# Streaming the columns of each linear product in one of seven orders

## The chip, the cores and the metric

One core of a Trainium2 chip runs the whole kernel. The metric is device time in microseconds. TensorE multiplies a stationary operand (128 x 128, loaded ahead of the matmul) with columns that are streamed from SBUF, and adds the result in PSUM. VectorE, ScalarE and GpSimd work beside it, and SyncE's queue starts most DMA transfers.

## What is computed

Three layers on a sequence of 256 tokens with 2048 features, all in float32: a block with stick-breaking attention and a gated delta rule, cross-attention to a memory and a convolutional feed-forward part; then a block with forgetting attention; then one with windowed attention. Between them stand normalisations and residual additions. Nearly all the arithmetic is in products of the hidden state with weight matrices:

```python
h = rmsnorm(x, mix_norm[l])
proj = h @ w_in[l]
...
x = x + mixed @ w_out[l]
...
u = causal_dwconv(h @ w_up, conv_w) + conv_b
gate, up = jnp.split(u, 2, axis=-1)
return (jax.nn.silu(gate) * up) @ w_down
...
p = h @ fox_w_in[j]
```

## The kernel before

The hidden state lies transposed in SBUF (`XT`, features on partitions, 256 tokens along the free axis). A float32 operand is split in two parts that TensorE takes in one pass each: a rounded high part and the rest, the low part. For x, `split` (line 211) leaves both in one tile `mv[P, 2, 256]`: high in `mv[:, 0, :]`, low in `mv[:, 1, :]`. For the weights, `granules` (line 242) loads blocks of up to four k-tiles of 256 weight columns by SyncE's queue into `wt`, lets ScalarE round them (line 262) and VectorE subtract (line 263), and hands out high and low weights of one k-tile after the other. It calls `tick` after each block of k-tiles, which lets waiting side work (attention, norms, the delta rule) put its own instructions between.

`linB` (line 270) makes one product of 256 output columns. For each k-tile and each half `j` of the 256 columns it issues a pair of matmuls. The first holds the high weights still and streams 512 columns: x high and x low, into `ps[:, j]`, which is one PSUM bank of 2 x 256 words. The second holds the low weights still, streams the 256 columns of x high, and adds them to the second half of the same bank, `ps[:, j, 1, :]`. The two halves are added when the result leaves PSUM (`scaled`, line 290, or `residual`, line 339). The accumulator `ps` has two buffers in turn. Most products have 16 k-tiles, so 32 pairs; those with `w_down` have 11, those with `w_xo` 4.

`linA` (line 280) does the same with x stationary and the weights streamed. The change does not touch it.

Instructions stand on each engine in the order in which the program text issues them; no planner moves them. Every matmul goes through `mm` (line 139), so all of them carry line 140 in the profile (`PE ... L140`), and VectorE's helpers carry lines 151 and 154. Groups are therefore told apart by the tiles they read and write: `linb<-xh,w` is a product of `linB` on the normalised hidden state, `linb<-mv,w`, `linb<-mix,w` and `linb<-mm,w` are those on other inputs.

A few smaller places are named below. `scores` (line 1048) makes the attention scores `zps` from `kd` and `qs`; its last matmul streams two runs of 128 columns that lie 256 apart, the other two stream 256 in a row. Line 604 makes `kq` with streamed columns in two runs of 64; `gbc` (line 599) streams 128 in a row. In `head`, line 768 makes `zps<-bset,identb`, writing 256 columns of PSUM as two runs of 128 that lie 256 apart. Lines 655 to 661, in the loop over `LEVELS = (2, 4, 8, 16, 32)`, write tile `X` from `xps` on VectorE: 128 elements of each partition, in runs of 2, 4, 8, 16 or 32 by the level, at both ends.

Of the kernel before, what the change touches and what calls it, by code (L numbers as in the profile page):

```python
# [24 lines left out]
FFC = 11  # L25
ROT = [(i + 8) % 16 if i < 16 else i for i in range(32)]
LEVELS = (2, 4, 8, 16, 32)

def _consts():
# [15 lines left out]
    parts["m0c"] = (q64 == r64 + 1) & (r64 % 2 == 0)  # L47
    for b in LEVELS:
        m = (r64 // (2 * b) == q64 // (2 * b)) & ((r64 // b) % 2 == 1) & ((q64 // b) % 2 == 0)
# [74 lines left out]
def body(ctx: ExitStack, tc: tile.TileContext, d: dict, out: bass.AP, stop=None):  # L124
# [14 lines left out]
    def mm(o, lhsT, rhs, start, stop):  # L139
        nc.tensor.matmul(o, lhsT, rhs, start=start, stop=stop, skip_group_check=True)  # L140

    def side(shape, name):
        t = pside.tile([P, 512], F32, tag="side", name=name)
        n = int(np.prod(shape[1:]))
        v = t[:, :n]
        if len(shape) == 3:
            v = v.rearrange("p (a b) -> p a b", a=shape[1])
        return v

    def tt(o, a, b, op):  # L150
        vec.tensor_tensor(o, a, b, op=op)  # L151
# [29 lines left out]
    ps = side([P, 2, P], "warm")  # L181
# [43 lines left out]
    def tick():  # L225

        for lane, width in WIDTH.items():
            for gen in list(lanes.get(lane, ()))[:width]:
                if next(gen, "end") == "end":
                    lanes[lane].remove(gen)  # L230
# [11 lines left out]
    def granules(w, runs, c0, first=(), inner=False):  # L242

        flat = []
        for r0, mvs in runs:
            g = 0
            for n in first:
                flat.append((r0 + g, mvs[g : g + n]))
                g += n
            for g in range(g, len(mvs), KG):  # L250
                flat.append((r0 + g, mvs[g : g + KG]))
        for gi, (r, mvs) in enumerate(flat):
            wt = wp.tile([P, len(mvs), 256], F32, tag="wt", name="wt", bufs=NWT)
            assert c0 % 256 == 0
            src = w[c0 // 2 : c0 // 2 + P, r * 256 : (r + len(mvs)) * 256].rearrange("p (k n) -> p k n", n=256)
            nc.sync.dma_start(wt[:], src)
            for h in range(0, len(mvs), KC):
                n = min(KC, len(mvs) - h)
                part = [mv() if callable(mv) else mv for mv in mvs[h : h + n]]
                w2 = wp.tile([P, n, 2, 256] if inner else [P, 2, n, 256], F32R, tag="w2", name="w2", bufs=NWC)  # L260
                wh, wl = (w2[:, :, e, :] if inner else w2[:, e] for e in range(2))
                act(wh, wt[:, h : h + n, :], AF.Copy)  # L262
                tt(wl, wt[:, h : h + n, :], wh.bitcast(F32), ALU.subtract)
                for i in range(n):
                    last = gi == len(flat) - 1 and h + i == len(mvs) - 1
                    both = w2[:, i] if inner else w2[:, :, i, :]
                    yield both, part[i], gi == 0 and h + i == 0, last
                tick()

    def linB(w, runs, c0, first=()):  # L270

        ps = pl.tile([P, 2, 2, 256], F32, tag="lin", name="linb")
        for w2, mv, first, last in granules(w, runs, c0, first):
            for j in range(2):
                c = slice(j * P, (j + 1) * P)
                mm(ps[:, j], w2[:, 0, c], mv[:], first, False)
                mm(ps[:, j, 1, :], w2[:, 1, c], mv[:, 0, :], False, last)
        return ps

    def linA(w, runs, c0):  # L280

        ps = pl.tile([P, 2, 2, 256], F32, tag="lin", name="lina")
        for w2, mv, first, last in granules(w, runs, c0, inner=True):
            for r in range(2):
                c = slice(r * P, (r + 1) * P)
                mm(ps[:, r], mv[:, 0, c], w2, first, False)
                mm(ps[:, r, 1, :], mv[:, 1, c], w2[:, 0, :], False, last)
        return ps
# [89 lines left out]
    def residual(w, runs, scale=1.0, after=None):  # L378

        for n in range(0, KT, 2):  # L380
            ps = linB(w, runs, n * P)
            xt = XT[:, n : n + 2, :]
            for e in range(2):
                stt(xt, ps[:, :, e, :], scale, xt, ALU.mult, ALU.add)
            if after is not None:
                after(n)
                after(n + 1)
# [149 lines left out]
    def gdn(hp):  # L537
        nonlocal r1, c1
        KQ = gd.tile([P, 2, 2, 256], F32, tag="KQ", name="KQ")
        if hp:  # L540
            for qk, seg in ((1, 0), (0, 1)):
                silu(KQ[:, qk], conv(linB(win, [(0, xh)], 3072 + 1024 * seg + 256 * hp), 8 * seg + 2 * hp))
        else:
            pq = linB(win, [(0, xh)], 3072, (2, 2, 4, 4, 4))
            norm0 = Norm("mix")
            later("norm", squares(norm0))
            r1 = norm0.rstd(0)
            pk = linB(win, [(0, xh)], 4096, (4, 4))
            nc.sync.dma_start(cols[:, 16:], d["cols"][:, 16:])
            tg = thin(d["w_gates"], V("mix_norm"))  # L550
        ps = linB(win, [(0, xh)], 5120 + 256 * hp)
        if hp == 0:
            silu(KQ[:, 1], conv(pq, 0))
            silu(KQ[:, 0], conv(pk, 8))
            nc.sync.dma_start(cst[:], d["consts"])
            late_constants()
            c1 = column(r1)
            later("gdn", make_gates(tg))
        v = conv(ps, 16 + 2 * hp)
        silu(v[:], v)  # L560
        ps = linB(win, [(0, xh)], 6144 + 256 * hp)
        z = t2("y", "z", 2)
        scaled(z[:], ps, r1)
        sz = t2("sz", "sz", 2)
        silu(sz[:], z)
        later("gdn", chain(hp, KQ, v, sz))

    def chain(hp, KQ, v, sz):
# [70 lines left out]
        act(T[:], tps, AF.Copy)  # L639
        for b in LEVELS:  # L640
            nb = 32 // b
# [6 lines left out]
            def product(lhsT, rhs, name):  # L648
                ps = side([P, 4, 64], name)
                for u in range(4):  # L650
                    for f in range(2):
                        mm(ps[HALF[f], u], lhsT[HALF[f], u], rhs[HALF[f], u], u == 0, u == 3)
                return ps
# [9 lines left out]
            nps = product(X, TT, "nps2")  # L663
            if b != LEVELS[-1]:
                mps = product(TT, X, "mps")
# [127 lines left out]
    def new_mv():  # L793
        return mvbox[0].tile([P, 2, 256], F32R, tag="mv", name="mv")
# [25 lines left out]
    with tc.tile_pool(name="xa", bufs=2) as xa_:  # L820
# [51 lines left out]
        for n in range(2):  # L872
            ps = linB(wkv, [(0, mmv)], n * 256)
# [33 lines left out]
    with tc.tile_pool(name="ff", bufs=2) as ff_:  # L907
# [15 lines left out]
        for n in range(22):  # L923
# [6 lines left out]
            for j in range(2):  # L930
                mv = new_mv()
# [96 lines left out]
    def halves(src, tag, bufs):  # L1028

        st = [ap_.tile([P, 2, 256], F32R, tag=f"{tag}{e}", name=tag, bufs=bufs) for e in range(2)]  # L1030
        for e in range(2):
            act(st[e][HALF[e]], src[HALF[e]], AF.Copy)
        for e in range(2):
            tt(st[e][HALF[1 - e]], src[HALF[e]], st[e][HALF[e]].bitcast(F32), ALU.subtract)
        return st
# [82 lines left out]
    for gidx in range(8):  # L1118
        c0 = 256 * gidx
        q = ap_.tile([P, 2, 256], F32, tag="qk", name="q")  # L1120
        k = ap_.tile([P, 2, 256], F32, tag="qk", name="k")
        vr = ap_.tile([P, 2, 256], F32, tag="v", name="v", bufs=1)
        ps = linB(wfx, [(0, xh)], c0)
        scaled(q[:], ps, r5, 0.125)
        q = halves(q, "qs", 1)
        if gidx == 0:
            c5 = column(r5)
        ps = linB(wfx, [(0, xh)], 2048 + c0)
# [11 lines left out]
        ps = linA(wfx, [(0, xh)], 4096 + c0)  # L1140
# [15 lines left out]
    def roped(ps, scale, tag):  # L1156
        qs = ap_.tile([P, 2, 256], F32, tag="gp", name="qs")
        scaled(qs[:], ps, r6, scale)
        rp = ap_.tile([P, 2, 256], F32, tag="rp", name="rp", bufs=1)
        vec.stream_shuffle(rp[:].rearrange("p a b -> p (a b)"), qs[:].rearrange("p a b -> p (a b)"), ROT)  # L1160
        o = ap_.tile([P, 2, 256], F32, tag=tag, name="ro")
        t = rp
        gps.tensor_tensor(t[:], rp[:], L("sin").unsqueeze(1).to_broadcast([P, 2, 256]), op=ALU.mult)
        tt(o[:], qs[:], L("cos").unsqueeze(1).to_broadcast([P, 2, 256]), ALU.mult)
        tt(o[:], o[:], t[:], ALU.add)
        return o
# [16 lines left out]
    ps = linA(wsw, [(0, xh)], 2304)  # L1183
    rows_scaled(lambda r: vr[:, r, :], ps, c6)
    ymv = [None] * KT
    for gidx in range(8):
        kvh = gidx // 2
        q = halves(roped(linB(wsw, [(0, xh)], 256 * gidx), 0.125, "qk"), "qs", 1)
# [59 lines left out]
def build(arrays, stop=None):  # L1248
    import concourse.bacc as bacc

    nc = bacc.Bacc("TRN2", target_bir_lowering=False, num_devices=1)
    d = {n: nc.dram_tensor(f"in_{n}", a.shape, F32, kind="ExternalInput").ap() for n, a in arrays.items()}
    out = nc.dram_tensor("out_0", (D, S), F32, kind="ExternalOutput").ap()
    with tile.TileContext(nc) as tc:
        body(tc, d, out, stop)
    return nc
# [9 lines left out]
```

## Time and profile before

| | us |
|---|---|
| median of 2 runs | 2259.31 (2258.99 to 2259.64) |
| the profiled execution's own time | 2261.78 |
| its span, first to last instruction | 2259.7 |
| TensorE busy (matmuls) | 2222.3 (98%) |
| TensorE weight loads, beside them | 1913.9 (85%) |
| VectorE busy | 1612.5 (71%) |
| ScalarE busy | 1256.9 (56%) |
| GpSimd busy | 113.6 (5%) |
| mean granted TensorE clock | 0.992 of full speed |

A matmul's busy time in the profile runs from its start to the end of its result, and successive matmuls overlap; so the mean duration of one is longer than its share of the stream. The pace is read from a stretch of many matmuls, divided by their number. Shapes are partitions x elements of a partition. Times are us unless marked ns.

### The profile page before, as it was taken

The page shows a single profiled execution, that of the slowest core. Times are in us where ns is not written, and L with a number is a line of the kernel's source. Part 1 is how long each engine was busy: PE and PEld are TensorE (multiplying, and loading weights), DVE is VectorE, ACT ScalarE, POOL GpSimd, SP SyncE. Part 2 cuts the span into 40 slices and gives each one's busy share as a digit, 9 for nine tenths or more (in the row PEclk, how much of TensorE's full clock was granted, in tenths as well). Part 3 has the DMA queues.
Part 4 walks back from the last instruction along what each step waited for, and adds up shares of the span by engine and source line. Part 5 has one row for each costly group of instructions (what it writes and reads, how often), then busy time and mean ns, then how long its engine had stood idle before and what let it go on. Part 6 is the DMA issues. An engine that isn't in the chain of part 4 may idle for free.

```text
span 2259.7 us, 35514 instructions
## 1 busy us (share of the span) xinstructions
PE 2222.3 (98%) x13582; PEld 1913.9 (85%) x13582; DVE 1612.5 (71%) x2681; ACT 1256.9 (56%) x2149; POOL 113.6 (5%) x161
## 2 busy tenths in 40 slices
PE   9999999999999999999999999999999999999997
PEld 7888888878878888888888888888888888888886
DVE  8756666467687766766775778867677666788775
ACT  7554555355565545544553556656565655577652
POOL 1100010000000000000000000000011000000011
PEclk9999999999999999999999999999999999999999
DMA  7443444346546666666566666555555555545453
GB/s 250 146 141 120 137 137 142 121 133 203 177 142 187 184 188 188 187 181 190 187 181 193 186 180 183 179 168 167 172 169 169 164 178 186 160 148 165 155 162 121
DMA packets 110265, 380.06 MB, mean 168 GB/s; under 512 B 11920, under 2 KB 18192, under 8 KB 110096
## 3 DMA queue, kind: packets, MB, share of 16 engines
q1 hardware_dynamic: 108720, 375.96, 54.1%
q8 instruction: 106, 1.74, 0.3%
q10 hardware_dynamic: 1232, 1.06, 0.1%
q0 software_dynamic: 144, 0.79, 0.1%
q14 instruction: 63, 0.52, 0.1%
HBM read 375.66 MB, written 2.10 MB: 167 GB/s over the span
## 4 chain that ended last, share of the span: by engine, by line
PE 92%; DVE 4%; ACT 2%; DMA 1%; issue 1%; POOL 0%; SPq 0%; DVEq 0%; ACTq 0%; POOLq 0%
PE linb L140 77%; PE lina L140 7%; PE zps L140 2%; PE yps L140 1%; DVE w L151 1%; PE ptps L993 1%; PE nps L140 1%; PE wsp L140 1%; DVE XT L154 1%; PE xps L140 1%; ACT w L262 1%; PE snp L140 0%; DMA wt<-in_fox_w_in 0%; PE mps L140 0%; DVE y L154 0%
## 5 line engine op out<-in xcount | busy, mean ns | idle before, releaser
L140 PE MATMUL linb<-xh,w 128*128 128x512 f32 x7104 | 1302.4, 342 | 11.0 <-DVE xh L154 2.9
L140 PEld LDWEIGHTS linb<-xh,w 128*128 128x128 f32 x7104 | 1098.6, 189 | 175.8 <-issue 4.7
L151 DVE TENSOR_TENSOR w<-wt,w 128x1024 fp32r<-128x1024 f32 (+2 forms) x713 | 869.0, 1221 | 334.9 <-ACT w L262 332.2
L262 ACT ACTIVATE w<-wt 128x1024 fp32r<-128x1024 f32 (+2 forms) x713 | 744.3, 1045 | 604.7 <-PE linb L140 443.6
L140 PE MATMUL linb<-mv,w 128*128 128x256 f32 (+1 forms) x2560 | 458.4, 340 | 4.2 <-DVE XT L154 4.1
L140 PEld LDWEIGHTS linb<-mv,w 128*128 128x128 f32 x2560 | 393.8, 188 | 65.0 <-issue 4.1
L140 PE MATMUL lina<-w,xh 128*128 128x512 f32 x832 | 155.4, 342 | 0.7 <-DVE w L151 0.7
L140 PEld LDWEIGHTS lina<-w,xh 128*128 128x128 f32 x832 | 128.0, 188 | 19.3 <-DVE w L151 0.9
L154 DVE SCALAR_TENSOR_TENSOR XT<-linb,XT 128x512 f32<-128x512 f32 x128 | 87.9, 690 | 32.6 <-PE linb L140 30.5
L154 DVE SCALAR_TENSOR_TENSOR y<-pre,cols,y 128x256 f32<-128x256 f32 x248 | 103.3, 479 | 0.2 <-ACT y L523 0.2
L140 PE MATMUL linb<-mix,w 128*128 128x512 f32 (+1 forms) x512 | 95.7, 347 | 1.9 <-DVE mix L151 1.9
L140 PEld LDWEIGHTS linb<-mix,w 128*128 128x128 f32 x512 | 80.8, 193 | 14.3 <-DVE mix L151 2.1
L292 ACT ACTIVATE pre<-linb 128x512 f32<-128x512 f32 x56 | 33.5, 598 | 97.2 <-PE linb L140 97.1
L154 DVE SCALAR_TENSOR_TENSOR pre<-linb,pre 128x512 f32<-128x512 f32 x56 | 38.6, 690 | 49.8 <-ACT pre L292 49.8
L917 ACT ACTIVATE y<-pre,cols 128x256 f32<-128x256 f32 x88 | 48.2, 595 | 26.8 <-DVE pre L151 26.8
L1045 POOL CAST kd<-kd 64x512 fp32r<-64x512 f32 x32 | 32.7, 1022 | 353.9 <-PE lina L140 322.9
L151 DVE TENSOR_TENSOR sqacc<-sqacc,sq 128x256 f32<-128x256 f32 x118 | 48.3, 420 | 1.4 <-DVE fg L151 0.5
L912 POOL MEMSET pre<- 128x4 f32 x44 | 4.3, 103 | 881.8 <-DVE y L154 667.2
L334 ACT ACTIVATE sq<-XT 128x256 f32<-128x256 f32 x90 | 35.5, 404 | 15.1 <-DVE XT L154 12.8
L151 DVE TENSOR_TENSOR pre<-pre,rstd 128x512 f32<-128x512 f32 x56 | 38.8, 692 | 1.6
L217 ACT ACTIVATE xh<-XT,cols 128x256 fp32r<-128x256 f32 x64 | 31.0, 500 | 10.0 <-DVE XT L154 8.8
L140 PE MATMUL zps<-kd,qs 128*128 128x256 f32 x192 | 31.3, 295 | 0.5 <-DVE qs L151 0.5
(300 smaller groups left out, 1575.5 us busy)
## 6 DMA issues: line engine op xcount, KB each, us to landing
wt<-in_w_up SPq DMA_DIRECT2D x176, 512.0 KB, 3.8
wt<-in_fox_w_in SPq DMA_DIRECT2D x128, 512.0 KB, 3.9
wt<-in_w_in SPq DMA_DIRECT2D x111, 512.0 KB, 3.7
wt<-in_swa_w_in SPq DMA_DIRECT2D x72, 512.0 KB, 4.3
wt<-in_w_down SPq DMA_DIRECT2D x64, 512.0 KB, 3.9
wt<-in_w_out SPq DMA_DIRECT2D x32, 512.0 KB, 4.2
wt<-in_fox_w_out SPq DMA_DIRECT2D x32, 512.0 KB, 3.7
wt<-in_swa_w_out SPq DMA_DIRECT2D x32, 512.0 KB, 4.4
```

Source lines behind the costliest of these rows:

```text
L140: nc.tensor.matmul(o, lhsT, rhs, start=start, stop=stop, skip_group_check=True)
L151: vec.tensor_tensor(o, a, b, op=op)
L154: vec.scalar_tensor_tensor(o, a, s, b, op0=op0, op1=op1)
L217: act(mv[:, 0, :], src, AF.Copy, scale=scale)
L262: act(wh, wt[:, h : h + n, :], AF.Copy)
L292: act(dst, ps[:, :, 1, :], AF.Copy, scale=scale)
L334: act(sq[:], src, AF.Square, scale=scale)
L912: gps.memset(pre[:, :, 0:2], 0.0)
L917: act(y[:, j, :], pre[:, j, 0:256], AF.Identity, scale=cw[:, c : c + 1], bias=cb[:, c : c + 1])
L993: nc.tensor.transpose(tps[:, b * P : b * P + P], p[:, b * P : b * P + P], ident)
L1045: gps.tensor_copy(st[e][other, i], st[e][own, i])
```

## The change

Every product of `linB` takes the next of seven orders in turn (the first takes the second of the list). The first entry of the list leaves the operands as they were. An order `(b, e)` makes both the streamed columns and the place in PSUM where they go run through `b` regions in turn, `e` columns of each at a time. With `b` = 2 the regions of the 512-column matmul are x high and x low; with `b` = 4 they are the halves of each. For the 256-column matmul the regions are the halves or quarters of x high. Since operand and output are rearranged alike, each column meets its own place in PSUM as before.

```diff
+ORDERS = (None, (2, 16), (2, 32), (2, 8), (2, 64), (4, 16), (2, 4))
...
+    turn = [0]
+
+    def next_order():
+        turn[0] += 1
+        return ORDERS[turn[0] % len(ORDERS)]
+
+    def ordered(ap, order):
+
+        if order is None:
+            return ap
+        b, e = order
+        if len(ap.shape) == 3 and b == 2:
+            return ap.rearrange("p a (q e) -> p q a e", e=e)
+        if len(ap.shape) == 3:
+            ap = ap.rearrange("p a n -> p (a n)")
+        return ap.rearrange("p (b q e) -> p q b e", b=b, e=e)
+
     def linB(w, runs, c0, first=()):
 
         ps = pl.tile([P, 2, 2, 256], F32, tag="lin", name="linb")
+        order = next_order()
         for w2, mv, first, last in granules(w, runs, c0, first):
             for j in range(2):
                 c = slice(j * P, (j + 1) * P)
-                mm(ps[:, j], w2[:, 0, c], mv[:], first, False)
-                mm(ps[:, j, 1, :], w2[:, 1, c], mv[:, 0, :], False, last)
+                mm(ordered(ps[:, j], order), w2[:, 0, c], ordered(mv[:, :, :], order), first, False)
+                mm(ordered(ps[:, j, 1, :], order), w2[:, 1, c], ordered(mv[:, 0, :], order), False, last)
         return ps
```

On TensorE, where the first product of the program ends and the second begins, the kernel before has these rows (`linb_104` and `linb_249` are the accumulators of the two products, `xh_...` the tile of x, `w2_...` the weights, and the last word the partitions and the streamed columns):

```order
L140 MATMUL linb_104<-xh_225,w2_228 128x512
L140 MATMUL linb_104<-xh_225,w2_228 128x256
L140 MATMUL linb_249<-xh_108,w2_252 128x512
L140 MATMUL linb_249<-xh_108,w2_252 128x256
L140 MATMUL linb_249<-xh_108,w2_252 128x512
```

The changed kernel has these in the same place:

```order
L142 MATMUL linb_104<-xh_225,w2_228 128x16x2x16
L142 MATMUL linb_104<-xh_225,w2_228 128x8x2x16
L142 MATMUL linb_249<-xh_108,w2_252 128x8x2x32
L142 MATMUL linb_249<-xh_108,w2_252 128x4x2x32
L142 MATMUL linb_249<-xh_108,w2_252 128x8x2x32
```

No row moved. The 512 columns became 16 x 2 x 16 (16 times, 16 columns of each of two regions) in the first product and 8 x 2 x 32 in the second.

On TensorE again, where the sixth product, with the shortest runs, ends and the seventh begins, with a step of the delta rule (`ttps`) between:

```order
L142 MATMUL linb_867<-xh_225,w2_971 128x64x2x4
L142 MATMUL linb_867<-xh_225,w2_971 128x32x2x4
L142 MATMUL linb_1020<-xh_108,w2_1023 128x512
L142 MATMUL ttps_957<-cst_81,TT_931 64x64 x8
L142 MATMUL linb_1020<-xh_108,w2_1023 128x256
```

The seventh product has the plain order, and its rows differ from those before only in the line number; the sixth streams runs of four columns.

## Rows read from the trace of the kernel before

**Rows 1.** the page: span, TensorE's busy time, the chain by engine and line

```profile
span 2259.7 us, 35514 instructions
...
PE 2222.3 (98%) x13582; PEld 1913.9 (85%) x13582; DVE 1612.5 (71%) x2681; ACT 1256.9 (56%) x2149; POOL 113.6 (5%) x161
...
PE 92%; DVE 4%; ACT 2%; DMA 1%; issue 1%; POOL 0%; SPq 0%; DVEq 0%; ACTq 0%; POOLq 0%
PE linb L140 77%; PE lina L140 7%; PE zps L140 2%; PE yps L140 1%; DVE w L151 1%; PE ptps L993 1%; PE nps L140 1%; PE wsp L140 1%; DVE XT L154 1%; PE xps L140 1%; ACT w L262 1%; PE snp L140 0%; DMA wt<-in_fox_w_in 0%; PE mps L140 0%; DVE y L154 0%
```

**Rows 2.** the table of waits, TensorE alone: us in total, times, longest

```profile
PE linb L140 <- DVE XT L154: 5.1, 4, 1.5
PE linb L140 <- DVE xh L154: 2.9, 3, 1.8
```

**Rows 3.** chain in order of time: start, us, engine, tile, matmuls

```profile
1488.12 8.48 PE lina L140 x48
...
1820.14 96.30 PE linb L140 x544
```

**Rows 4.** busy us (instructions) by engine for `linb`, granted clock, DMA, 900 to 1200 us

```profile
900.00:1200.00 300.00, 300.00 (x1697) 260.86 (x1697) 28.36 (x41) 11.38 (x19) 1.00 0.61 186
```

**Rows 5.** groups of TensorE by shape for `linb`: busy us, mean ns, idle before

```profile
L140 PE MATMUL linb<-xh,w 128*128 128x512 f32 x3552 | 1280.9, 401 | 8.7 <-DVE xh L154 2.9 <-DVE sbk L154 2.8 <-ACT w L262 2.0
...
L140 PE MATMUL linb<-xh,w 128*128 128x256 f32 x3552 | 1005.0, 283 | 2.3 <-DVE w L151 2.3
...
L140 PE MATMUL linb<-mv,w 128*128 128x512 f32 x1280 | 454.4, 397 | 4.2 <-DVE XT L154 4.1
...
L140 PE MATMUL linb<-mv,w 128*128 128x256 f32 x1280 | 360.5, 283 | 0.0
...
L140 PE MATMUL linb<-mix,w 128*128 128x512 f32 x256 | 93.5, 405 | 1.9 <-DVE mix L151 1.9
...
L140 PE MATMUL linb<-mix,w 128*128 128x256 f32 x256 | 73.7, 288 | 0.0
...
L140 PE MATMUL linb<-mm,w 128*128 128x512 f32 x64 | 23.3, 404 | 0.0
...
L140 PE MATMUL linb<-mm,w 128*128 128x256 f32 x64 | 18.0, 282 | 0.0
```

**Rows 6.** TensorE tiles: least/median/most ns, first and last start, shapes

```profile
L140 PE MATMUL zps<-kd,qs x192: 276/283/419, 1441.7 to 2157.1; 128*128 128x256 f32 x192
...
L140 PE MATMUL zps<-bset,identb x8: 272/273/273, 181.6 to 458.3; 128*128 128x256 bf16 x8
...
L140 PE MATMUL kq<-KQ x64: 272/273/324, 76.8 to 382.4; 128*64 128x128 f32 x64
...
L140 PE MATMUL gbc<-cst,g x32: 270/275/275, 75.8 to 381.4; 128*128 128x128 f32 x32
```

**Rows 7.** VectorE's writes of tile `X`, same columns

```profile
L151 DVE TENSOR_TENSOR X<-xps,cst x20: 283/292/298, 93.6 to 431.5; 128x128 f32<-128x128 f32 x20
```

**Rows 8.** plain fp32 matmuls of TensorE by shape: busy us, mean ns

```profile
L140 PE MATMUL zps<-sbq,sbk 128*128 128x256 f32 x16 | 5.1, 399 | 0.0
```

## The prediction

> **What bounds the kernel now.** I read the page first: TensorE is busy in 2222.3 us of a span of 2259.7 us, the next engine (VectorE) in 1612.5, and the chain of work that ended last runs over TensorE for 92% of the span, 77% of it in the products of `linb` [rows 1]. So whatever a `linb` product gains or loses is passed on to the end nearly one to one. The table of waits says the same from the other side: the longest wait of TensorE is 5.1 us in all, and all of its idle time is 2259.7 - 2222.3 = 37 us [rows 1, 2]. No other engine can give much and none can hide much.
>
> A busy TensorE is not yet TensorE at its peak, so next comes its pace. The chain in order of time shows whole runs of `linb` products: 544 matmuls in 96.30 us [rows 3]. They come in pairs (512 columns with the high weights, then 256 with the low), so a pair takes 96.30 / 272 = 354 ns. In a stretch that is dense with them the granted clock is 1.00 [rows 4], which is the level of 2.4 GHz, and 512 + 256 columns at one a cycle are 320 ns. So 34 ns in each pair, about a tenth, are not columns; the trace doesn't say what they are. Groups by shape give the number of pairs: 3552 + 1280 + 256 + 64 = 5152 [rows 5]. That is 5152 x 354 ns = 1824 us, the bulk of the kernel.
>
> **The change, part by part.** It adds and removes no instruction. The order of the two programs is the same row by row on every engine, DMA issues included, and so is what each waits for; only the shape of the two matmuls of a pair differs. One product in seven keeps the plain order. Counted in the built program, 736 pairs keep it and 4416 get a new one. A new order reads the same columns from SBUF and writes the same columns in PSUM, but in short runs that jump between two (or four) regions: with `(2, 16)` 16 columns of the high half of x, then 16 of the low half. Every run is followed by a jump on the read side and one on the write side. The number of runs in a pair is 768 / e:
>
> - `(2, 16)` 48 runs x 748 pairs = 35,904
> - `(2, 32)` 24 x 744 = 17,856
> - `(2, 8)` 96 x 736 = 70,656
> - `(2, 64)` 12 x 726 = 8,712
> - `(4, 16)` 48 x 726 = 34,848
> - `(2, 4)` 192 x 736 = 141,312
>
> In sum 309,288 runs, of which the shortest order has 46%. All depends on one price, that of a jump, and the trace of before has no matmul with so many. I bound it by what is there.
>
> From TensorE itself: line 1051 (the last matmul of `scores`) reads its 256 columns as two runs of 128, beside two matmuls that read 256 in a row. The three are one group with 276/283/419 ns as least, median and most; the plain 256-column matmul of `linb` has a mean of 283 [rows 5, 6]. `kq` reads 128 columns as two runs of 64 and has a median of 273 ns, where `gbc` reads 128 in a row in 275 [rows 6]. And `zps<-bset,identb` writes its 256 columns in two runs of 128 that lie apart in PSUM: 272/273/273 [rows 6]. So a jump in the read or in the write costs nothing there that can be seen. But these have one jump, at 64 columns or more, and durations of a pipelined matmul don't show a cycle or two.
>
> From VectorE, far away but with short runs: the loop over `LEVELS` writes `X` from `xps` five times for each block of heads, always 128 elements, in runs of 2, 4, 8, 16 and 32, read from PSUM and written in SBUF. All 20 lie between 283 and 298 ns [rows 7]. From 64 runs to 4 the spread is at most 15 ns, so at most 15 / 60 = 0.25 ns a run. This is a slower engine, and 128 elements in some 290 ns leave it room that TensorE at a column each cycle doesn't have.
>
> So the price of a jump lies between 0 (TensorE's own rows) and 0.25 ns (VectorE's), which is 0 to 309,288 x 0.25 ns = 77 us. I take 0, since the nearest rows are those of TensorE. For a gain the bound is the 34 ns that are no columns: if an order took all of them away, 4416 x 34 ns = 150 us. Nothing in the trace ties them to the order of reading, so I take 0 here as well.
>
> One thing could be worse than a jump: the low matmul adds to columns that the high one has just written. In the plain order each is written 256 columns before it is added to. In the new ones the distance is 256 or more, and 240 at the least with `(4, 16)`, so no such wait appears.
>
> [...]
>
> The sum: the profiled execution took 2261.8 us (span 2259.7 and 2.1 around it), 2.5 above the median of the runs, 2259.3, which is 0.1%. Changes: 0 for instructions, 0 for jumps, 0 for the 34 ns. **I predict 2260 us.**
>
> **The rivals.**
>
> *Each jump costs a cycle (slower).* TensorE takes in a column each cycle; if its address generator, the SBUF read or the PSUM write loses one at every run, that is 0.417 ns x 309,288 = 129 us, 2389 us in all, with 59 us of it from `(2, 4)` alone. It decides from 45 us (2%), which is 0.15 ns a run or a third of a cycle. For it: the 34 ns in a pair show that the stream isn't free of losses already. Against it: `kq` and the `scores` group [rows 6].
>
> *Short runs stream at half rate (slower).* The records of plain fp32 matmuls show a slower stream on the same engine: 256 columns take 399 ns where `linb` takes 283, so 116 ns more for 256 columns [rows 5, 8]. With that price a pair costs 3 x 116 = 348 ns more. If it hits `(2, 4)` alone, 736 x 348 ns = 256 us and 2516 us in all; if it hits all six orders, 4416 x 348 ns = 1537 us, about 3800. For it: the `linb` stream takes a column each cycle and plain fp32 does not, so it has the least room for a pattern that is harder to read. Against it: the same group, and VectorE's indifference to runs of 2 [rows 6, 7]. [...]
>
> *The jumps help (faster).* If the 34 ns come from reading and writing one region for long, alternating between regions 1 KB apart could give some back: 150 us at most, 2110 in all; with a third of it 2210. For it: only that the 34 ns have no explanation. Against it: `lina`, which streams the weights past stationary x and so reads other tiles, has the same pace, 48 matmuls in 8.48 us, 353 ns a pair [rows 3]; a loss that hung on the place would not be the same in both.
>
> That the change is none is excluded: the built program has the new shapes.
>
> **How the numbers follow.** No change to be seen 0.62; a cost of the order of a cycle a run 0.19; half rate for some or all orders 0.12; a gain 0.07. The price at which a slowdown is over 2% splits the second case little, since a third of a cycle is enough; I put 0.02 of it and 0.01 of the gain back to "within 2%". So faster 0.06, same 0.65, slower 0.29; 2% is about what a measurement of this kernel can tell from no change. For the range I leave out the gain (0.07) below and half rate (0.12) above, and take in VectorE's bound (2337) and the cycle a run (2389): 2245 to 2395. The likeliest case alone is 2250 to 2270.
>
> **What the profile after would show.** If I am right, runs of `linb` in the chain keep 354 ns a pair whatever the order, the group means stay near 401 and 283 ns, and TensorE's busy time near 2222. If jumps cost, the pace splits by product: plain ones stay at 354 ns, `(2, 64)` grows least and `(2, 4)` most, in proportion to the runs (a cycle each) or only at the short end (half rate); ScalarE and VectorE would idle longer on `linb`. If it is a gain, the pairs of the new orders fall towards 320 ns. I am also wrong, in a way that none of the rivals covers, if the granted clock in dense stretches is no longer 1.00.

## The result, and the profile after

The changed kernel takes 2291.81 us (median of 2 runs, 2291.31 to 2292.30) where the one before takes 2259.31: a ratio of 1.0144, 95% interval 1.0100 to 1.0187, or 32.5 us more. That is below 2% and clear of no change. The page of its profile, with the lines that answer to [rows 1]:

```profile
span 2289.4 us, 35514 instructions
...
PE 2253.0 (98%) x13582; PEld 1924.0 (84%) x13582; DVE 1613.0 (70%) x2681; ACT 1261.2 (55%) x2149; POOL 113.7 (5%) x161
...
PE 94%; DVE 3%; ACT 2%; issue 1%; DMA 1%; POOL 0%; SPq 0%; DVEq 0%; ACTq 0%; POOLq 0%
```

As many instructions as before; the span grew by 29.7 us, TensorE's busy time by 30.7, VectorE's by 0.5. So the time was lost inside TensorE's stream and came out at the end nearly whole, as its share of the chain says. The dense stretch from 900 to 1200 us shows the same (columns as in [rows 4]):

```profile
900.00:1200.00 300.00, 300.00 (x1667) 258.30 (x1666) 26.30 (x38) 12.04 (x20) 1.00 0.59 182
```

1667 matmuls where [rows 4] has 1697, TensorE busy all the time in both, and the granted clock 1.00 in both: it isn't the clock.

Now the price of each order. The layer with forgetting attention has a place that comes once for each group of heads, where the chain shows 16 pairs of one product without a break. A group has three products of `linB`, so the order at this place goes on by three of seven, and seven groups show all seven orders. In order of time (start, us, engine, tile, matmuls), they are plain, `(2, 8)`, `(2, 4)`, `(2, 32)`, `(4, 16)`, `(2, 16)`, `(2, 64)`:

```profile
1521.23 5.65 PE linb L142 x32
...
1571.79 5.87 PE linb L142 x32
...
1622.44 6.08 PE linb L142 x32
...
1673.78 5.71 PE linb L142 x32
...
1724.61 5.63 PE linb L142 x32
...
1775.75 5.76 PE linb L142 x32
...
1826.82 5.65 PE linb L142 x32
```

Before, the chain has the same place seven times with 5.65 us each, the first of them

```profile
1501.56 5.65 PE linb L140 x32
```

so the place itself doesn't change from group to group. Divided by 16 pairs, and with the runs of a pair and the steps that the outermost of the three loops of the pattern takes (the runs divided by the regions):

| order | runs | outer steps | ns a pair | more than plain |
|---|---|---|---|---|
| plain | | | 353.1 | |
| `(2, 64)` | 12 | 6 | 353.1 | 0 |
| `(2, 32)` | 24 | 12 | 356.9 | 3.8 |
| `(2, 16)` | 48 | 24 | 360.0 | 6.9 |
| `(2, 8)` | 96 | 48 | 366.9 | 13.8 |
| `(2, 4)` | 192 | 96 | 380.0 | 26.9 |
| `(4, 16)` | 48 | 12 | 351.9 | -1.2 |

With two regions the price about doubles as the runs get half as long, 0.14 to 0.16 ns a run; `(2, 64)` is free, and so is `(4, 16)` with as many runs as `(2, 16)`. Times the pairs of each order (748, 744, 736, 726 ... as in the prediction) this gives 2.8 + 5.2 + 10.2 + 19.8 - 0.9 = 37 us; the busy time grew by 30.7. Part of the other 6 us is the clock of the two profiles. Over the same products, from 413 to 654 us before (first line) and from 418 to 658 us after (second), the mean granted clock, the third figure from the end, was 0.97 before and 0.99 after, so the changed kernel's profile lost less to the clock there:

```profile
413.00:654.00 241.00, 231.76 (x1375) 197.58 (x1374) 155.93 (x250) 128.03 (x234) 0.52 (x5) 0.97 0.50 155
...
418.00:658.00 240.00, 231.62 (x1369) 195.88 (x1369) 155.66 (x248) 128.44 (x233) 0.51 (x5) 0.99 0.50 155
```

What is left of the 6 us is not traced.

### The profile page after: what moved, and what is told of

Read it like the earlier page. It is cut to its first block, busy times and chain, and to the rows that moved or that the text cites. A ratio compares the mean times of both kernels' runs of the same rounds, so it can differ in the third digit from the quotient of the medians.

```text
span 2289.4 us, 35514 instructions
## 1 busy us (share of the span) xinstructions
PE 2253.0 (98%) x13582; PEld 1924.0 (84%) x13582; DVE 1613.0 (70%) x2681; ACT 1261.2 (55%) x2149; POOL 113.7 (5%) x161
## 4 chain that ended last, share of the span: by engine, by line
PE 94%; DVE 3%; ACT 2%; issue 1%; DMA 1%; POOL 0%; SPq 0%; DVEq 0%; ACTq 0%; POOLq 0%
PE linb L142 78%; PE lina L142 7%; PE zps L142 2%; PE yps L142 1%; PE ptps L1013 1%; PE nps L142 1%; DVE w L153 1%; PE wsp L142 1%; PE xps L142 1%; DVE XT L156 0%; ACT w L264 0%; PE snp L142 0%; PE mps L142 0%; PE sbo L142 0%; DMA wt<-in_w_in 0%
## 5 line engine op out<-in xcount | busy, mean ns | idle before, releaser
L142 PE MATMUL linb<-xh,w 128*128 128x512 f32 x7104 | 1325.3, 346 | 10.0 <-DVE xh L156 3.2
L142 PE MATMUL linb<-mv,w 128*128 128x256 f32 (+1 forms) x2560 | 466.2, 344 | 4.0 <-DVE XT L156 4.0
L1001 ACT ACTIVATE p<-p,stats 128x256 f32<-128x256 f32 x64 | 31.9, 499 | 0.0
```

Of the source, the lines that this page charges most:

```text
L1001: act(p[:, 128:384], p[:, 128:384], AF.Exp, bias=nm[:, 1:2], scale=-1.0, accum_out=sm[:, 1:2])
```

## The experiments

One stretch of the chain serves as a yardstick for all kernels: the eight products with `fox_w_out` but for their first 16 matmuls (496), and the first 48 matmuls of the product behind them, 544 matmuls or 272 pairs without a break. Before it took 96.30 us [rows 3], 354 ns a pair, and in the changed kernel, with all seven orders in it:

```profile
1843.64 98.37 PE linb L142 x544
```

or 362 ns. Times of runs below are those of a single execution unless an interval is given; the kernel before took 2257.2, 2259.5, 2258.1 and 2258.5 us in the four groups of runs that follow.

### Is the price paid where columns are read, or where sums are written?

`natural` gives a tile the loops of the order without its jumps, so that the two sides of a matmul agree in shape. First only the reads jump:

```diff
-ORDERS = (None, (2, 16), (2, 32), (2, 8), (2, 64), (4, 16), (2, 4))
+ORDERS = ((2, 4),)
...
-                mm(ordered(ps[:, j], order), w2[:, 0, c], ordered(mv[:, :, :], order), first, False)
-                mm(ordered(ps[:, j, 1, :], order), w2[:, 1, c], ordered(mv[:, 0, :], order), False, last)
+                mm(natural(ps[:, j], order), w2[:, 0, c], ordered(mv[:, :, :], order), first, False)
+                mm(natural(ps[:, j, 1, :], order), w2[:, 1, c], ordered(mv[:, 0, :], order), False, last)
```

> Every product of linB reads its columns in the order (2, 4), but writes them to PSUM in the plain order, so columns land in wrong places of the accumulator and the values are not those of the reference; instructions, sizes and waits are unchanged. In the changed kernel a pair of matmuls in the order (2, 4) takes 380 ns where a plain pair takes 353. Theory READ (the jump is paid where the columns are fetched from SBUF): pairs at 380 ns here, 5152 x 27 ns = 139 us more than before, about 2398 us. Theory WRITE (it is paid where the sums go to PSUM): pairs at 353 ns, about 2260 us. Both sides share it: in between, near 2330 us.

Then only the writes:

```diff
+                mm(ordered(ps[:, j], order), w2[:, 0, c], natural(mv[:, :, :], order), first, False)
+                mm(ordered(ps[:, j, 1, :], order), w2[:, 1, c], natural(mv[:, 0, :], order), False, last)
```

> The counterpart: every product reads its columns in the plain order and writes them to PSUM in the order (2, 4); values land in wrong places as well. READ: pairs at 353 ns, about 2260 us. WRITE: pairs at 380 ns, about 2398 us. Shared: near 2330 us.

And both, with nothing but the list of orders changed to `((2, 4),)`:

> Every product uses the order (2, 4) for reading and writing, with right values. If the price hangs on the order alone, and not on the change of orders from product to product, 5152 pairs x 27 ns = 139 us more than before, about 2398 us. If the slow pairs of the changed kernel were slow for their place in the program, fewer.

Measured: 2384.33, 2259.86 and 2383.47 us. The yardstick in the chain, reads only:

```profile
1916.65 103.56 PE linb L142 x544
```

writes only:

```profile
1818.26 96.30 PE linb L142 x544
```

both:

```profile
1915.94 103.56 PE linb L142 x544
```

So the reads pay all of it (103.56 us, 381 ns a pair) and the writes nothing: 96.30 us to the hundredth, as in the plain order, with 192 jumps in each of 5152 pairs on the PSUM side. READ holds and WRITE and the shared price fall, for the order `(2, 4)`; for the other orders the two sides were not tried apart. "Both" stayed 15 us below the 2398 expected: 2383.5 - 2257.2 = 126 us are 24.5 ns for each of 5152 pairs, a little less than the 27 of an unbroken stream.

### Runs, steps of the outer loop, or distance?

`(4, 16)` for every product:

```diff
+ORDERS = ((4, 16),)
```

> Every product uses the order (4, 16). Its 48 runs in a pair are as many as those of (2, 16), whose pairs took 360 ns in the changed kernel. Theory of a price per run (0.14 ns, from (2, 4), (2, 8) and (2, 16)): 360 ns, 5152 x 7 = 36 us more, about 2296 us. The trace of the changed kernel itself shows 351 ns for the pairs in (4, 16), 2 below the plain ones: by that 5152 x 2 = 10 us less, about 2250 us, which would beat both kernels. If it is the distance of 1 KB between the two regions that costs, (4, 16) with 512 B costs nothing: 2260 us.

Measured: 2251.47 us, ratio 0.9968 (0.9957 to 0.9980), that is a little faster than before. Its yardstick:

```profile
1811.51 95.61 PE linb L142 x544
```

351.5 ns a pair. A price that is the same for each run, whatever the order, is refuted, as the trace of the changed kernel had it.

`(4, 4)`, as many runs as `(2, 4)` with half the outer steps:

```diff
+ORDERS = ((4, 4),)
```

> Every product uses the order (4, 4): 192 runs of 4 columns in a pair, as in (2, 4), but through four regions, 512 B apart in the 512-column matmul and 256 B in the other, where (2, 4) has 1 KB and 512 B; the outer of the three loops of the pattern steps 48 times in a pair and not 96. Theory RUN (each jump of the read costs about 0.14 ns): pairs at 380 ns, about 2383 us. Theory WRAP (each step of the outermost loop costs 0.28 ns): 353 + 48 x 0.28 = 366 ns, about 2320 us. Theory DISTANCE (reads that return to an address 1 KB or 512 B away in the next run collide, nearer ones don't; (4, 16) was free): 353 ns or less, about 2255 us.

Measured: 2500.80 us, slower than each of the three theories said:

```profile
2009.45 109.46 PE linb L142 x544
```

402 ns a pair, 48 more than plain. RUN (380) and WRAP (366) fall as they stand, and so does DISTANCE in the form that nearer regions are free: 512 B and 256 B can cost more than 1 KB does.

The same number of runs with jumps of 32 B: 64 regions for the 512 columns and 32 for the 256, so that a first pass reads every other 16 B and a second pass the rest.

```diff
+ORDERS = ((64, 4),)
...
-                mm(ordered(ps[:, j, 1, :], order), w2[:, 1, c], ordered(mv[:, 0, :], order), False, last)
+                mm(ordered(ps[:, j, 1, :], (32, 4)), w2[:, 1, c], ordered(mv[:, 0, :], (32, 4)), False, last)
```

> Every product reads runs of 4 columns (16 B) and skips the next 16 B, through the whole operand, and comes back for the skipped ones: 192 runs in a pair again, but jumps of 32 B from start to start, and the outermost loop steps 4 times. RUN: 380 ns a pair, about 2383 us. WRAP: 354 ns, about 2260 us. DISTANCE: 353 ns or less, about 2257 us; if fetching works on pieces longer than 16 B that hold both the read and the skipped run, each is fetched twice and the pair is slower than 380 ns.

Measured: 2236.68 us, *faster* than before by 1%. I ran it again, several times, on another chip:

> The kernel that reads 16 B and skips 16 B again, timed in rounds. If its one look (2236.7 us, pairs at 347 ns) was no accident of that chip: 0.990 of the kernel before, about 2235 us, and pairs at 347 ns. If it was, 1.0.

Measured: 2232.18 us against 2258.11, ratio 0.9882 (0.9866 to 0.9899). TensorE's busy time on its page (2222.3 before):

```profile
PE 2192.6 (98%) x13582; PEld 1897.6 (85%) x13582; DVE 1611.1 (72%) x2681; ACT 1256.8 (56%) x2149; POOL 113.7 (5%) x161
```

and the yardstick:

```profile
1797.20 94.50 PE linb L142 x544
```

347.4 ns a pair. Three kernels with 192 runs of 4 columns in a pair thus take 402, 381 and 347 ns. At equal length and number of runs, it is not the jump as such that costs; the patterns differ in where the next run lies and in their outer steps. The distance alone doesn't settle it either: `(4, 16)` jumps between the same regions as `(4, 4)` and is free.

Next, which of the two matmuls pays. Only the 512-column one jumps, with the list of orders `((2, 4),)` as in "both":

```diff
+                mm(ordered(ps[:, j], order), w2[:, 0, c], ordered(mv[:, :, :], order), first, False)
+                mm(ps[:, j, 1, :], w2[:, 1, c], mv[:, 0, :], False, last)
```

> Only the 512-column matmuls use the order (2, 4), with regions 1 KB apart; the 256-column ones, where (2, 4) means 512 B, keep the plain order. Theory KILOBYTE (a return to an address 1 KB away costs one cycle of 2.4 GHz, 64 x 0.417 = 27 ns for each high matmul): the whole price stays, pairs at 380 ns, about 2383 us. Theory HALF (512 B costs as well, 0.28 ns for each step of the outer loop in either matmul): 64 of 96 steps are left, pairs at 353 + 18 = 371 ns, about 2342 us. If the low matmul pays alone: 353 ns, 2259 us.

Measured: 2379.73 us, and the yardstick

```profile
1913.37 103.50 PE linb L142 x544
```

against 103.56 for both: the matmul whose regions are 1 KB apart brings the whole price by itself when the other one is plain. It doesn't follow that the 256-column matmul pays nothing in "both". The groups by shape put the durations so, first "both", then only the 512-column matmul with jumps (before: 401 and 283 ns [rows 5]):

```profile
L142 PE MATMUL linb<-xh,w 128*128 128x512 f32 x3552 | 1371.1, 420 | 6.3 <-DVE sbk L156 2.8 <-DVE xh L156 2.4 <-DVE XT L156 1.0
L142 PE MATMUL linb<-xh,w 128*128 128x256 f32 x3552 | 1046.1, 295 | 1.4 <-DVE w L153 1.4
...
L142 PE MATMUL linb<-xh,w 128*128 128x512 f32 x3552 | 1368.3, 428 | 6.9 <-DVE sbk L156 2.8 <-DVE xh L156 2.7 <-DVE XT L156 1.0
L142 PE MATMUL linb<-xh,w 128*128 128x256 f32 x3552 | 1005.8, 283 | 1.6 <-DVE w L153 1.6
```

In "both" the 512-column matmul is 19 ns longer than before and the other 12; alone, the first is 27 ns longer and the other 0. These are durations of matmuls that overlap, so they don't add up to the pair; but the pair pays the same, by another division.

What a cycle is worth shows in a stage of the kernel before where the granted clock was 0.50 (second line, third figure from the end). There the chain takes 2.56 us for four plain pairs, 640 ns a pair or 0.833 ns a column:

```profile
14.27 2.56 PE linb L140 x8
...
14.27:16.83 2.56, 2.56 (x10) 0.50 1.05 408
```

Halved for a clock of 1.00 this is 0.417 ns a column and 320 ns for the 768 columns of a pair, an estimate that takes the pace of columns to go with the clock. A cycle here means these 0.417 ns.

The 64 outer steps of the 512-column matmul at 0.417 ns are 26.7 ns, and 32, 16 and 8 steps are 13.3, 6.7 and 3.3; the table has 26.9, 13.8, 6.9 and 3.8. So a cycle for each return to an address 1 KB away has the size of the price of the two-region orders (only `(2, 64)`, 1.7 by this rule, shows 0); that the division in "both" is another speaks against it as the whole account. So do two pairs in the order `(2, 4)` of the changed kernel at a granted clock of 0.50, which take 640 ns each, as the plain ones do at that clock:

```profile
573.24 1.28 PE linb L142 x4
...
573.24:574.51 1.27, 1.27 (x5) 0.50 0.73 232
```

To test the distance itself, 32 B of space between the high and the low half of x, all else as in "both":

```diff
-        mv = xp.tile([P, 2, 256], F32R, tag="xh", name="xh")
+        mv = xp.tile([P, 2, 264], F32R, tag="xh", name="xh")[:, :, 0:256]
```

(and alike for the tiles `mv`, `mm` and `mix`).

> The kernel with the order (2, 4) in every product, but each tile of x has 32 B of space between its high and its low half: the two regions of the 512-column matmul lie 1056 B apart and not 1024. Runs, jumps and steps of the outer loop are as many, the low matmul is unchanged. Theory KILOBYTE (a cycle is lost when a read returns to an address exactly 1 KB away): pairs fall from 380 to 353 ns or less, about 2258 us. Theory STEP (a pattern of two regions loses a cycle at every step of its outer loop wherever they lie): 380 ns, about 2382 us. The smaller run of weight tiles against more space for x changes nothing else.

Measured: 2326.82 us. The yardstick, and a product of `linA`, which has no order:

```profile
1531.22 8.36 PE lina L142 x48
...
1871.31 100.22 PE linb L142 x544
```

368 ns a pair: neither 353 nor 380. With the same loops and as many runs, 1056 B instead of 1024 takes 12 of the 27 ns away, so the address matters; some 14 stay, so it isn't 1 KB exactly that costs. And the space did something that I hadn't counted: `linA`, which reads x as weights, went from 8.48 us [rows 3] to 8.36, 353 to 348 ns a pair, with nothing changed for it but where tiles lie. The test is not as clean as I meant it: the plain order with the space was not run, so it may be that part of the 12 ns is a gain of any order from the new places, and not of the distance between the two regions.

### Does the weight load share in it?

Each load reads one column 128 times:

```diff
-                mm(ordered(ps[:, j], order), w2[:, 0, c], ordered(mv[:, :, :], order), first, False)
+                mm(ordered(ps[:, j], order), w2[:, 0, j * P : j * P + 1].to_broadcast([P, P]), ordered(mv[:, :, :], order), first, False)
```

(the low weights alike), first with plain order, then with `(2, 4)`.

> Plain order, but each weight load reads one column 128 times in place of 128 columns (values are not those of the reference), so the load reads one address per partition and not 512 B. Of the 353 ns of a plain pair 33 are no columns at 2.4 GHz. Theory LOAD (they are lost where the reads of a weight load meet the reads of the streamed columns): pairs near 320 to 330 ns, 25 to 33 ns less, about 2100 to 2130 us. Theory OWN (the stream loses them by itself or in the handover of weights): 353 ns, about 2257 us.

> The order (2, 4) for every product together with those one-column weight loads. LOAD, if the price of short runs comes from meeting the weight load too: as fast as the plain order with such loads. If short runs cost by themselves, whatever the load reads: 27 ns a pair or about 126 us more than the plain order with such loads, as with full loads (2383 against 2257).

Measured: 2228.27 and 2365.85 us. Plain, then `(2, 4)`:

```profile
1791.65 94.50 PE linb L142 x544
```

```profile
1902.29 102.35 PE linb L142 x544
```

347.4 and 376.3 ns a pair. One-column loads give back 6.6 of the 34 ns, so LOAD, which had 25 to 33, holds for a fifth of them. The rest stays with such loads; OWN is what is left for it, and no run shows its source. And they leave `(2, 4)` its price: 28.9 ns more with them, 26.7 without. The order `(2, 4)` costs its price whatever the load reads.

The gain of one-column loads has the size of the gain of the 16 B skip. Both together:

> The order that reads 16 B and skips 16 B, together with weight loads that read one column 128 times (values are not those of the reference). Each alone brought a pair from 353 to 347 ns. Theory SAME (both take away the meeting of the two reads): 347 ns again, about 2230 us. Theory ADD (two separate losses): 341 ns, 5152 x 6 = 31 us less, about 2200 us.

Measured: 2233.67 us.

```profile
1797.56 94.49 PE linb L142 x544
```

347 ns again, nothing on top. SAME holds in its number: the two gains don't add. That the skip works by keeping the stream away from the reads of the load is the simplest reading, and `linA` in the kernel with the space points there too; it is argued from sizes, not shown.

## Why the prediction was right and where it was wrong

The forecast (2260 us, within 2%, 2245 to 2395) held in its class and range: 1.4% slower, 2291.8. The likeliest case alone, 2250 to 2270, missed. That it stayed within 2% was luck of the mix and not the mechanism: the sum had the jumps at 0, and with `(2, 4)` in every product the same sum would have been 5.6% short (2383.47 against 2257.16 us).

**What bounds the kernel** held. TensorE's stream took the loss and passed it on; the busy times of the other engines stayed within 5 us [rows 1].

**Nothing but shapes changed** held: as many instructions, and TensorE's idle time is 2289.4 - 2253.0 = 36 us, 37 before.

**"I take 0" for a jump** is the step that failed. Averaged over 309,288 runs the price is 32.5 us / 309,288 = 0.105 ns, inside the bound of 0.25 that the rows of VectorE gave, and not at its lower end. The reason that I gave was that TensorE's own rows are the nearest. They have one jump at runs of 64 or 128 columns [rows 6], and that case is free in the changed kernel as well: `(2, 64)`, 353.1 ns. What they could not say is how the price grows as runs get shorter, from 3.8 to 26.9 ns. Extending "free" from one jump to 64 was the error, and I had written beside it that durations of a pipelined matmul hide a cycle or two: 64 such cycles of 0.417 ns would be 26.7 ns.

**Reads and writes as one** was too coarse. The sum counted jumps on both sides with one price. The writes cost nothing in `(2, 4)`, where the two were tried apart; it was all in the reads.

**0 for the 34 ns** failed too, the other way. The 34 ns stand on 320 ns for the columns of a pair. In the trace they are an estimate: half of the 640 ns measured at a granted clock of 0.50, or 0.417 ns a column, which is the one a cycle of 2.4 GHz that I reckoned with. I wrote that nothing ties them to the order of reading. An order does give 6.6 of them back, and the kernel that uses it everywhere beats the one before by 1.2%. The order `(4, 16)` alone is worth 0.3%.

**The rival of a cycle for each jump** had the engine right and the SBUF read among its three places, and was four times too dear: the two-region orders lost about a cycle (26.9 ns for 64 steps, 13.8 for 32) for each step of the outer loop in the 512-column matmul, a third of their runs, and `(2, 64)` and `(4, 16)` lost nothing. Its marks in the profile (plain pairs stay, `(2, 4)` grows most, in proportion) are those of the table. **Half rate** did not appear in the changed kernel; the worst order that I tried, `(4, 4)`, adds 48 ns where half rate would add 348. **The gain** was there for `(4, 16)`, with 1 to 3 ns a pair. `linA` at 353 ns spoke against a loss that hangs on the place, I wrote; in the kernel with the space it moved to 348 with nothing changed for it but where tiles lie.

**What stays open**: the rule by which addresses cost. One cycle per return at 1 KB fits the two-region orders at a clock of 1.00, not `(2, 64)`, and not `(2, 4)` at 0.50; it gives no account of `(4, 4)`, nor of the 14 ns that stay at 1056 B, nor of why in `(2, 4)` the low matmul is 12 ns longer while the pair pays no more than with a plain one, nor of why `(4, 4)` pays most where `(4, 16)`, between the same regions, pays nothing. It would take other distances, reads and writes apart in the other orders, and the plain order with the tiles moved. Some 27 ns of a pair (347 less the estimated 320) are left by the fastest kernels here and not explained.

## What to carry to other kernels

Where TensorE's stream was the bound, as here (92% of the chain [rows 1]), the pattern in which it took its columns was a cost of its own: two patterns with equal run length and equal count differed by 16% in the pace of a pair (402 against 347 ns), so price a pattern by a run on the chip, and don't infer it from a row with one jump. On the PSUM side runs of four columns that alternate between two regions cost nothing (96.30 us with them and without); other patterns of writing were not tried by themselves. The pace here lay a tenth above the estimate for the columns (354 against 320 ns a pair), and of the orders tried the one that takes 16 B and skips 16 B gave 1.2% for a few lines of code.

## What the runs showed of the hardware that I had not expected

- Matmuls that take every other 16 B of the columns first and the rest in a second pass, reading and writing, ran faster than those that go straight through: 347.4 against 354 ns a pair. Which of the two sides gains was not tried apart.
- Weight loads that read a single column have an effect of the same size, 347.4 ns, and the two don't add. So what a weight load reads bears on the stream, by 6.6 ns in a pair with two loads, though the loads lie beside the matmuls: on the page of the kernel before they are busy for 85% of the span and the matmuls for 98% [rows 1].
- Writing PSUM in runs of four columns that alternate between places 1 KB or 512 B apart cost nothing, to the hundredth of a us in 96.30.
- 32 B more between the two halves of a tile went with a pace that was 12 ns a pair faster in one pattern, and 5 ns faster in products that read this tile as weights.
